# Delta rule: decay factors from running sums in zero-padded rows, values and gated outputs transposed by VectorE and through DRAM

## The chip, the cores and the metric

The kernel runs on one core of one Trainium2 chip. The metric is device time in microseconds (us), the median over runs of the whole program. Before the change it is 2708.5 us (three runs, 2707.7 to 2711.6). Engines are named as in the profile: PE is TensorE, PEld its weight load, DVE is VectorE, ACT is ScalarE, POOL is GpSimd, SP is SyncE, which issues nearly all DMAs. Line numbers (L354) are those of the kernel before; in the changed kernel they are a little different (the helper `tr`, L363, is L364 there, and `dma`, L367, is L368).

## The reference

Two pre-norm residual layers over 256 tokens of width 2048, all in float32. Layer 0 has stick-breaking attention as its mixer, layer 1 a gated DeltaNet; a SwiGLU FFN with 5632 hidden columns follows each. The change is in the second mixer:

```python
proj = h @ w_in                                   # q, k: 16 heads; v, z: 32 heads of 128
qkv, z, b, a = jnp.split(proj, [...], axis=-1)
qkv = jax.nn.silu(causal_dwconv(qkv, conv_w))     # 4 taps along the tokens, per channel
q, k = l2_norm(q) * dh ** -0.5, l2_norm(k)        # 16 heads, each used by two value heads
beta = jax.nn.sigmoid(b)
g = -jnp.exp(a_log) * jax.nn.softplus(a + dt_bias)
# in chunks, g the running sum inside a chunk:
decay = jnp.where(causal, jnp.exp(g[:, None] - g[None, :]), 0.0)
a_mat = strict_lower((k * beta) @ k.T * decay);  t_mat = inverse(a_mat + eye)
u, w = t_mat @ (v * beta), t_mat @ (k * beta * jnp.exp(g))
v_new = u - w @ state
out = (q * jnp.exp(g)) @ state + (q @ k.T * decay) @ v_new
state = state * jnp.exp(g_last) + (k * jnp.exp(g_last - g)).T @ v_new
o = rms_norm(out, o_norm) * jax.nn.silu(z)
y = o @ w_out
```

The kernel uses chunks of 128 tokens, so there are two (t = 0 and 1).

## The kernel before, in words

All 256 tokens stay on the chip. x is held as 128 tokens x 512 columns tiles; activations that feed a product are held transposed (channels on the partitions, 256 tokens along the row) as a pair hi, lo in the rounded type fp32r, with hi + lo the float32 value. Weights are streamed once from DRAM in *units* of two k-tiles (128 x 1024). SP loads a unit into a raw buffer, ScalarE writes its hi part, VectorE subtracts to get its lo part (L328, L332, tile `w`), and TensorE makes three products for each k-tile and half of the tokens: hi x hi, hi x lo, lo x hi. In the profile these are two matmuls on `w,hTh` and one on `w,hTl` (on `kh`, `kl` where the operand is an attention or FFN output), 128x512 each, into one of the accumulators `acc`. A block of 512 output columns over 16 k-tiles is 96 such matmuls. The FFNs use a seven-product scheme for part of their columns, with conversions of 128 x 1792.

**Order.** The program is one list in an order that the code plans itself; engines run their own part of it in sequence and wait on semaphores. The planner keeps a planned time for each engine (`self.t`). Weight blocks form the main stream; everything else is a *task*, a generator that does some instructions and yields. Before each group of three stream matmuls `tick` steps those tasks whose earlier instructions are done by the planned times, unless ScalarE or VectorE is planned more than `LAG` us past TensorE (`LAG7` in the FFN's seven-product part). `spend` adds an instruction's planned duration, `transfer` that of a DMA; `later` and `nap` postpone a task's next step. Nothing of these times exists on the chip: they only fix the order. `GDN_ORDER` lists the mixer's blocks: ('qk', g), ('v', g), ('z', g) for the eight groups g of four value heads, ('ba',) for the gates, ('out', a, b) for the product of heads a to b with w_out.

**Transposes.** There are two ways. `tr` (L363) lets TensorE transpose 128x128 by a product with the identity, into a PSUM bank. `turn` (L891) lets VectorE transpose a 128x512 tile in 32x32 blocks in place (STREAM_TRANSPOSE), writes it to a DRAM buffer `way` with stores of 32 partitions, and loads it back with two DMAs so that the blocks come out in their transposed places. If the two tiles lie side by side, four stores and two loads do; otherwise eight and two. Before, `turn` serves q and k of the attention and half of the norms (`TURNED`), and a like routine, `turned_pairs`, the FFN's hidden columns.

**The mixer's tasks, by group.** `gdn_qk`: evacuate, transpose on TensorE, convolve. `gdn_v`: evacuate two tiles (one for each t), transpose them by eight `tr` in two banks, convolve from the bank. `gdn_z`: evacuate, then Silu on z and on the convolved values; `gdn_values` transposes the values back. `gdn_scores` makes k k^T and k q^T, and multiplies them by the decay factors E that `gdn_decay` makes (which = 0 and 2: between positions of the first and of the second chunk; 1: from the start of the second chunk). `gdn_blocks32` and `gdn_inverse` invert, through DRAM scratch. `gdn_finish` applies all this to the values, normalises, multiplies by Silu(z) and has `transposed_pairs` turn the result (eight `tr` in two banks) and split it into `kh`, `kl` for the out blocks.

**Decay factors before.** `gdn_gates` puts g, token by token on the partitions, into `ghl` (hi and lo). For each group and t, VectorE multiplies the triangular mask `upto` by each head's g (tile `gm`, hi and lo, 128x512), and TensorE multiplies by the strict triangle `after` (or by ones for which = 1): six 128x512 matmuls for each group, which give the sums of g between two positions. ScalarE takes the exponential.

**Norm into the FFN.** `norm_part` transposes new x columns (by `tr` or `turn`), scales them into `hTh` and `hTl`, and spawns `norm_stats`, the squares of x (`slab<-x` on ScalarE). hTh_65 to hTh_79 (odd) and hTl_66 to hTl_80 are two k-tiles each; hTh_69 and hTl_70 hold k-tiles 4 and 5, of the second 512 columns.

Of the kernel before, what the change touches and what calls it, by code (L numbers as in the profile page):

```python
# [15 lines left out]
P = 128  # L16
D = 2048
S = 256
# [139 lines left out]
class Trunk:  # L158
# [16 lines left out]
    LAG = 2.0  # L175
# [9 lines left out]
    GDN_ORDER = [('qk', 0), ('ba',), ('v', 0), ('qk', 1), ('z', 0), ('v', 2), ('v', 1), ('z', 1), ('qk', 2), ('qk', 3), ('v', 3), ('z', 2), ('z', 3), ('out', 0, 4), ('out', 4, 8), ('qk', 4), ('v', 4), ('qk', 5), ('v', 5), ('z', 5), ('z', 4), ('qk', 7), ('v', 6), ('qk', 6), ('out', 8, 16), ('v', 7), ('z', 6), ('z', 7), ('out', 16, 24), ('out', 24, 32)]  # L185

    def __init__(self, ctx, tc, ins, out):
# [26 lines left out]
        self.scratch = [dram.tile(s, F32, name=f"scratch{k}") for k, s in enumerate(([32, 1024], [8, P * (P + 1)]))]  # L214
# [138 lines left out]
    def mm(self, out, lhsT, rhs, start=True, stop=True, after=0.0):  # L353
        self.nc.tensor.matmul(out, lhsT, rhs, start=start, stop=stop, skip_group_check=True)  # L354
# [64 lines left out]
    def more_constants(self):  # L419
# [16 lines left out]
        self.after = t("after", [P, P], F32R)  # L436
# [34 lines left out]
        self.copy(self.after, aft)  # L471
# [113 lines left out]
    def product(self, u):  # L585
        b, (hi, lo, after) = u.block, u.conv
        ks = range(u.k0, u.k0 + u.nk)
        if b.kind == "ba":
            acc = b.acc[0]
            c = b.cols  # L590
            for k in ks:
                o = b.ops[k]
                wh, wl = hi[:, k * c:(k + 1) * c], lo[:, k * c:(k + 1) * c]
# [297 lines left out]
    def turn(self, parts, back=False, src=None):  # L891
# [8 lines left out]
        self.cur.later = self.TURN  # L900
# [7 lines left out]
        for a in range(4):  # L908
# [10 lines left out]
            self.cur.nap = self.STEP if a < 3 else None  # L919
# [361 lines left out]
    def gdn_blocks(self, norm, nxt, last):  # L1281
# [13 lines left out]
        self.gs = [dict(g=g, ops=heads[4 * g:4 * g + 4]) for g in range(8)]  # L1295
        z0 = 2 * KEY + VAL
# [25 lines left out]
    def gdn_gates(self, acc, free):  # L1322
# [31 lines left out]
        gt = w[:, :, 0, :]  # L1354
        for t in range(NT):
            self.stt(gt[:, t, :], zz[:, t, 1, :], -1.0, ea, ALU.mult, ALU.mult)
        self.ghl = self.sb("ghl", [P, NT, 2, HV], F32R)
        for t in range(NT):
            self.act(self.ghl[:, t, 0, :], gt[:, t, :])
            self.tt(self.ghl[:, t, 1, :], gt[:, t, :], self.ghl[:, t, 0, :].bitcast(F32), ALU.subtract)  # L1360
# [4 lines left out]
        yield  # L1365

        self.rest = self.sb("rest", [P, HV])
        self.act(self.rest, bank[:, :HV], AF.Exp)
# [424 lines left out]
```

## Time and profile before

| | us |
|---|---|
| median of three runs | 2708.5 (2707.7 to 2711.6) |
| the profiled execution | 2705.98 |
| its span, first to last instruction | 2704.3 |
| PE busy | 2669.4 |
| DVE busy | 2182.7 |
| ACT busy | 1491.8 |
| DMA, share of 16 engines' time on queue q1 | 67.1% |

The span has four stretches: attention to about 405 us, the first FFN to 1080, the DeltaNet mixer to about 1980, the second FFN to the end. A group of the profile reads: line, engine, operation, output tile <- input tiles, shapes, count | busy us, mean ns of one | idle us of that engine just before, and what ended it. Matmul durations overlap (a 128x512 matmul shows as some 390 ns while the next one starts sooner), so the price of a matmul is read from the starts in a timeline, not from its duration. A row of a timeline has start, length, engine, line, operation, tiles, shape, count. A row of waits has: who waited <- for whom: us in total, times, longest us. A row of DMA issues ends with count, KB of one, and the median us from issue to landing.

### The profile page before, as it was taken

The numbers are of one execution on the slowest core, as the hardware profiler recorded it, in microseconds if no ns is written. First come the engines' busy times: TensorE is split into PE (matmuls) and PEld (weight loads), VectorE is DVE, ScalarE is ACT, GpSimd is POOL, SyncE is SP. The second block draws the span as 40 slices with busy tenths as digits, with TensorE's granted clock in tenths as the row PEclk, the third lists the DMA queues.
The fourth block names the chain that finished last, engine by engine and source line by source line (L and its number), as shares of the span: only waits on it lengthen the run. The fifth ranks groups of instructions, "written<-read, shape, count | busy, mean of one in ns | idle before, by whom it ended". The sixth has DMA issues, their size and how long they took to land.

```text
span 2704.3 us, 39527 instructions
## 1 busy us (share of the span) xinstructions
PE 2669.4 (99%) x14730; PEld 2274.6 (84%) x14730; DVE 2182.7 (81%) x3451; ACT 1491.8 (55%) x1961; POOL 11.2 (0%) x95
## 2 busy tenths in 40 slices
PE   9999999999999999999999999999999999999999
PEld 7888888888888888888888888888878888888887
DVE  6556568899999897678778887887679899989885
ACT  6555556554555554565665556645575555555453
POOL 0000000000000000000000000000000000000000
PEclk9999999999999999999999999999999999999999
DMA  7766775787676777855656556556567767767776
GB/s 245 202 185 196 219 211 164 208 231 212 203 218 205 208 211 233 227 174 172 182 143 195 159 161 175 168 153 186 170 191 212 223 196 220 217 188 218 226 209 188
DMA packets 487611, 534.41 MB, mean 198 GB/s; under 512 B 188087, under 2 KB 267258, under 8 KB 487418
## 3 DMA queue, kind: packets, MB, share of 16 engines
q1 hardware_dynamic: 487370, 531.87, 67.1%
q8 instruction: 115, 1.88, 0.3%
q14 instruction: 78, 0.64, 0.1%
q10 hardware_dynamic: 48, 0.02, 0.0%
HBM read 508.20 MB, written 23.59 MB: 197 GB/s over the span
## 4 chain that ended last, share of the span: by engine, by line
PE 83%; DVE 10%; issue 2%; ACT 2%; DMA 2%; SPq 0%; ACTq 0%; DVEq 0%
PE acc L354 61%; PE bank L354 20%; DVE w L332 5%; DVE slabs L332 2%; PE bank L363 1%; DMA slab<-in_ffn_w_gu_dram 1%; ACT slabs L328 1%; ACT w L328 1%; DVE slab L338 1%; DVE slab L332 1%; DVE slab L939 1%; DMA slab<-in_ffn_w_down_dram 0%; ACT slab L328 0%; DVE x L332 0%; DMA w<-in_ffn_w_gu_dram 0%
## 5 line engine op out<-in xcount | busy, mean ns | idle before, releaser
L332 DVE TENSOR_TENSOR w<-w,w 128x1024 fp32r<-128x1024 f32 (+2 forms) x746 | 946.3, 1285 | 249.0 <-ACT w L328 247.6
L328 ACT ACTIVATE w<-w 128x1024 fp32r<-128x1024 f32 (+2 forms) x650 | 802.8, 1244 | 417.8 <-PE acc L354 347.0
L354 PE MATMUL acc<-w,hTh 128*128 128x512 f32 (+1 forms) x3232 | 925.0, 369 | 9.1 <-DVE w L332 8.4
L354 PEld LDWEIGHTS acc<-w,hTh 128*128 128x128 f32 x3232 | 585.9, 189 | 120.5 <-DVE w L332 14.5
L354 PE MATMUL acc<-w,hTl 128*128 128x512 f32 (+1 forms) x1616 | 590.2, 365 | 3.1 <-DVE hTl L338 3.1
L328 ACT ACTIVATE slabs<-slab 128x1024 fp32r<-128x1024 f32 x264 | 279.3, 1058 | 431.9 <-DMA slab<-in_ffn_w_gu_dram 123.8
L332 DVE TENSOR_TENSOR slabs<-slab,slabs 128x1024 fp32r<-128x1024 f32 x264 | 321.5, 1218 | 93.1 <-ACT slabs L328 93.1
L354 PE MATMUL acc<-w,kh 128*128 128x512 f32 x1184 | 369.6, 393 | 0.0
L354 PEld LDWEIGHTS acc<-w,hTl 128*128 128x128 f32 x1616 | 304.5, 188 | 53.5 <-DVE hTl L338 3.9
L332 DVE TENSOR_TENSOR w<-w 128x256 f32<-128x256 f32 (+1 forms) x576 | 291.2, 508 | 9.8 <-DMA w<-in_ffn_w_gu_dram 2.6
L354 PEld LDWEIGHTS acc<-w,kh 128*128 128x128 f32 x1184 | 218.8, 188 | 43.7
L354 PE MATMUL acc<-w,kl 128*128 128x512 f32 x592 | 230.7, 390 | 0.0
L354 PE MATMUL acc<-slabs,hTh 128*128 128x512 f32 x608 | 190.1, 392 | 2.8 <-DVE slabs L332 2.8
L354 PE MATMUL bank<-w,wide 128*128 128x256 f32 x1296 | 178.9, 283 | 0.0
L354 PEld LDWEIGHTS bank<-w,wide 128*128 128x128 f32 x1296 | 165.8, 192 | 0.0
L354 PE MATMUL bank<-slabs,hTh 128*128 128x512 f32 x512 | 159.9, 392 | 3.1 <-DVE slabs L332 3.1
L354 PE MATMUL bank<-slabs,kh 128*128 128x512 f32 x512 | 159.6, 392 | 3.4 <-DVE slabs L332 3.4
L354 PE MATMUL acc<-slabs,kh 128*128 128x512 f32 x480 | 149.9, 392 | 2.1 <-DVE slabs L332 1.9
L354 PEld LDWEIGHTS acc<-slabs,hTh 128*128 128x128 f32 x608 | 111.0, 188 | 25.1 <-DVE slabs L332 4.9
L354 PEld LDWEIGHTS acc<-w,kl 128*128 128x128 f32 x592 | 111.1, 188 | 23.4
L354 PE MATMUL acc<-slabs,hTl 128*128 128x512 f32 x304 | 118.3, 389 | 0.0
L328 ACT ACTIVATE slab<-bank 32x128 f32<-32x128 f32 (+4 forms) x181 | 67.9, 379 | 89.3 <-PE bank L354 87.1
(216 smaller groups left out, 2933.4 us busy)
## 6 DMA issues: line engine op xcount, KB each, us to landing
w<-in_ffn_w_gu_dram SPq DMA_DIRECT2D x212, 512.0 KB, 4.5
slab<-in_ffn_w_gu_dram SPq DMA_DIRECT2D x140, 512.0 KB, 4.5
w<-in_gdn_w_in_dram SPq DMA_DIRECT2D x129, 512.0 KB, 4.3
slab<-in_ffn_w_down_dram SPq DMA_DIRECT2D x124, 512.0 KB, 4.5
w<-in_sb_w_in_dram SPq DMA_DIRECT2D x96, 512.0 KB, 4.5
w<-in_gdn_w_in_dram SPq DMA_DIRECT2D x128, 256.0 KB, 3.7
w<-in_gdn_w_out_dram SPq DMA_DIRECT2D x64, 512.0 KB, 4.4
w<-in_ffn_w_down_dram SPq DMA_DIRECT2D x52, 512.0 KB, 5.5
```

The source lines that it names most:

```text
L328: self.nc.scalar.activation(out, in_, func, **kw)
L332: self.nc.vector.tensor_tensor(out, a, b, op=op)
L338: self.nc.vector.scalar_tensor_tensor(out, a, s, b, op0=op0, op1=op1)
L354: self.nc.tensor.matmul(out, lhsT, rhs, start=start, stop=stop, skip_group_check=True)
L363: self.nc.tensor.transpose(out, in_, self.ident[:p, :p])
L939: self.nc.vector.transpose(s, t)
```

## The change

- *Decay factors.* `gdn_gates` lets TensorE form the running sums of g themselves, once for all heads, in both layouts: tokens on partitions (`gsum`) and heads on partitions. The latter goes as a hi and a lo row per head to a DRAM scratch. For each group `gdn_decay` loads two rows of 512 (hi and lo of four heads) and copies them into rows 0 and 1 of the tile `gm`, whose other 126 rows stay zero; one matmul with ones (`onesr`) spreads hi + lo over all partitions. ScalarE then makes exp(-relu(gsum - sum)): one Relu for each head with `gsum` as bias, one Exp. The products of VectorE and four of six matmuls per group are gone. `after` and `ghl` are gone.
- *Values.* `gdn_v` uses `turn` and convolves from the loaded tiles. `evac_tok` asks for two tiles side by side.
- *Gated outputs.* `gdn_finish` uses `turn` for all groups but that of the last z block in GDN_ORDER (group 7), which keeps the TensorE transposes.
- *Planning.* LAG is 3.0 instead of 2.0; a 128x512 fp32r matmul outside of the seven-product part is planned at 512/2400 + 0.0135 us instead of + 0.006; GDN_ORDER is another; the norm's `turn` waits 0.2 us instead of 1.0 before its stores and 0.5 instead of 1.2 between them (`soon`).

```diff
-    LAG = 2.0
+    LAG = 3.0
-    GDN_ORDER = [('qk', 0), ('ba',), ('v', 0), ('qk', 1), ('z', 0), ('v', 2), ('v', 1), ('z', 1), ...
+    GDN_ORDER = [('v', 0), ('ba',), ('qk', 1), ('qk', 0), ('v', 1), ('z', 1), ('z', 0), ('qk', 2), ...
...
         if lhsT.dtype == F32R:
-            self.spend("pe", max(0.107, n / 2400 + 0.006), after)
+            over = 0.006 if self.seven else 0.0135
+            self.spend("pe", max(0.101 + over, n / 2400 + over), after)
...
     def norm_part(self, st, n):
-            yield from self.turn(parts, src=[self.x[t][n] for t in range(NT)])
+            yield from self.turn(parts, src=[self.x[t][n] for t in range(NT)], soon=True)
...
     def turn(self, parts, back=False, src=None, soon=False):
-        self.cur.later = self.TURN
+        self.cur.later = 0.2 if soon else self.TURN
...
-            self.cur.nap = self.STEP if a < 3 else None
+            self.cur.nap = (0.5 if soon else self.STEP) if a < 3 else None
...
     def gdn_gates(self, acc, free):
+        s = yield from self.slabs.get()
+        gt = s[:, :NT * 2 * HV].rearrange("p (t k h) -> p t k h", t=NT, k=2)
...
-        for hl in range(2):
-            self.mm(bank[:, :HV], self.after, self.ghl[:, 0, hl, :], start=hl == 0, stop=hl == 1)
+        for t in range(NT):
+            self.mm(bank[:, t * HV:(t + 1) * HV], self.upto, gt[:, t, 0, :])
+            self.mm(bank[:2 * HV, S + t * P:S + (t + 1) * P], gt[:, t, :, :].rearrange("p k h -> p (k h)"), self.upto)
+        self.mm(bank[:, 2 * HV:3 * HV], self.negones, gt[:, 0, 0, :])
...
+        for k in range(2):
+            self.dma(self.scratch[2][k].rearrange("t h i -> h t i"), s[k * HV:(k + 1) * HV, :S].rearrange("h (t i) -> h t i", t=NT))
...
     def gdn_decay(self, G):
-        for t, outs in ((0, (0,)), (1, (2, 1))):
-            gm = yield from self.gms.get()
-            for hl in range(2):
-                gb = self.ghl[:, t, hl, gsl].bitcast(F32).unsqueeze(2).to_broadcast([P, 4, P])
-                self.tt(h4(gm[hl]), up, gb, ALU.mult)
-            yield
-            for which in outs:
-                bank = yield from self.banks.get()
-                lhs = self.onesr if which == 1 else self.after
-                for hl in range(2):
-                    self.mm(bank, lhs, gm[hl], start=hl == 0, stop=hl == 1)
-                yield
-                e = yield from self.slabs.get()
-                self.act(e, bank, AF.Exp)
+        for t in range(NT):
+            s = yield from self.slabs.get()
+            self.dma(s[0:2, :].rearrange("p (h i) -> p h i", h=4), self.scratch[2][:, t, 4 * g:4 * g + 4, :])
+            rows.append(s)
+        yield
+        gm = yield from self.gms.get()
+        for t in range(NT):
+            self.act(gm[t][0:2, :], rows[t][0:2, :])
+        self.slabs.put(*rows)
+        yield
+        for t in range(NT):
+            bank = yield from self.banks.get()
+            self.mm(bank, self.onesr, gm[t])
+            yield
+            e = yield from self.slabs.get()
+            for h in range(4):
+                n = slice(h * P, (h + 1) * P)
+                self.act(e[:, n], bank[:, n], AF.Relu, scale=-1.0, bias=self.gsum[:, t, 4 * g + h:4 * g + h + 1])
+            self.act(e, e, AF.Exp, scale=-1.0)
+            G["E"][2 * t] = e
+            if t == 1:
+                e = yield from self.slabs.get()
+                self.act(e, bank, AF.Exp)
+                G["E"][1] = e
...
     def gdn_v(self, G, acc, free):
         toks = yield from self.evac_tok(acc, free)
-        vc = []
+        yield from self.turn(toks)
+        G["vc"] = vc = yield from self.two()
         for part in range(2):
-            s = yield from self.slabs.get()
-            vc.append(s)
-            bank = yield from self.banks.get()
-            for j in range(2):
-                for t in range(NT):
-                    self.tr(bank[:, j * S + t * P:j * S + (t + 1) * P], toks[t][:, (part * 2 + j) * P:(part * 2 + j + 1) * P])
-            yield
-            self.conv([(bank[:, j * S:(j + 1) * S], s[:, j * S:(j + 1) * S], 32 + g * 4 + part * 2 + j) for j in range(2)])
+            halves = [slice(j * S, (j + 1) * S) for j in range(2)]
+            self.conv([(toks[part][:, n], vc[part][:, n], 32 + g * 4 + part * 2 + j) for j, n in enumerate(halves)])
...
     def gdn_finish(self, G):
-        yield from self.transposed_pairs(G["z"], G["ops"], self.gains[:, 66:67])
+        if g in self.gs_last:
+            yield from self.transposed_pairs(G["z"], G["ops"], self.gains[:, 66:67])
+            return
+        yield from self.turn(G["z"])
+        for n, s in enumerate(G["z"]):
+            pair = yield from self.pairs.get()
+            self.operands_of(G["ops"][2 * n:2 * n + 2], pair, s.rearrange("p (k s) -> p k s", k=2), self.gains[:, 66:67])
+        self.slabs.put(*G["z"])
```

How the order moves is shown at three places. The first is PE, the decay matmuls of the first groups in the mixer, between the products of a weight block (`acc`) with the last k-tiles; first before, then with the change.

```order
L354 MATMUL bank_109<-gm_95,after 128x512
L354 MATMUL bank_109<-gm_96,after 128x512
L354 MATMUL acc_105<-w_123,hTh_79 128x512 x2
L354 MATMUL acc_105<-w_123,hTl_80 128x512
L354 MATMUL bank_110<-gm_95,onesr 128x512
L354 MATMUL bank_110<-gm_96,onesr 128x512
L354 MATMUL acc_106<-w_123,hTh_65 128x512 x2
```

```order
L354 MATMUL bank_109<-gm_95,onesr 128x512
L354 MATMUL acc_105<-w_124,hTh_79 128x512 x2
L354 MATMUL acc_105<-w_124,hTl_80 128x512
L354 MATMUL bank_111<-gm_96,onesr 128x512
L354 MATMUL acc_106<-w_124,hTh_65 128x512 x2
```

gm_95 and gm_96 were hi and lo of one sum and are now the two chunks t, so that a pair becomes a single matmul, and the pairs with `after` have gone.

The second is ACT at the entry into the first FFN, where hTh_69 is made from the turned x (`slab,nss<-x_63` are the squares for the norm, `wide` operands of the seven-product scheme); first before, then with the change.

```order
L328 ACTIVATE slab<-bank_110,gains 128x256 x2
L328 ACTIVATE w_123<-w_122 128x1024
L328 ACTIVATE wide_2481<-slab 128x512
L328 ACTIVATE w_124<-w_122 128x1024
L328 ACTIVATE slab,nss_140<-x_63 128x512 x2
L328 ACTIVATE hTh_69<-slab,gains 128x256 x2
L328 ACTIVATE hTh_71<-slab,gains 128x256 x2
```

```order
L328 ACTIVATE hTh_75<-bank_111,gains 128x256 x2
L328 ACTIVATE w_124<-w_123 128x1024
L328 ACTIVATE slab<-bank_111,gains 128x256 x2
L328 ACTIVATE hTh_69<-slab,gains 128x256 x2
L328 ACTIVATE hTh_71<-slab,gains 128x256 x2
L328 ACTIVATE wide_2477<-slab 128x512
```

The squares of x_63 stood directly ahead of hTh_69 and now come eight rows behind it.

The third is SP in the mixer, after the gates' transfers, with the change (before, loads of `w` and the transfers of the inverse were all that stood there). way_122 is the DRAM buffer of the first group's values, scratch_116 that of the running sums.

```order
L368 DMA way_122<-slab 32x32x32
L518 DMA w_123<-in_gdn_w_in_dram 128x2x256 x2
L368 DMA way_122<-slab 32x32x32
L368 DMA scratch_116<-slabs 32x2x128 x2
L368 DMA way_122<-slab 32x32x32
L518 DMA w_123<-in_gdn_w_in_dram 128x2x256 x2
L368 DMA way_122<-slab 32x32x32
L518 DMA w_7759<-in_gdn_w_in_dram 128x2x256 x2
L518 DMA w_123<-in_gdn_w_in_dram 128x2x256 x2
L368 DMA slab<-way_122 128x4x128 x2
L518 DMA w_123<-in_gdn_w_in_dram 128x2x512 x3
```

Four stores and two loads of a turn now stand between the weight loads, and SP takes them in this sequence. The like happens for the other 14 turns.

More of the change, by code (lines that the diff above doesn't have):

```diff
@@ L213, in __init__ @@
         dram = ctx.enter_context(tc.tile_pool(name="scratch", bufs=1, space=bass.MemoryType.DRAM))
-        self.scratch = [dram.tile(s, F32, name=f"scratch{k}") for k, s in enumerate(([32, 1024], [8, P * (P + 1)]))]
+        self.scratch = [dram.tile(s, F32, name=f"scratch{k}") for k, s in enumerate(([32, 1024], [8, P * (P + 1)], [2, NT, HV, P]))]
         self.ways = Slots([dram.tile([NT * NB, P], F32, name=f"way{k}") for k in range(6)])
@@ L592, in product @@
                 o = b.ops[k]
+                if not o.ready:
+                    self.until(lambda: o.ready, ("operand", b.name, k))
                 wh, wl = hi[:, k * c:(k + 1) * c], lo[:, k * c:(k + 1) * c]
@@ L889, in two, with turn @@
         return [a, b]
-    def turn(self, parts, back=False, src=None):
+    def turn(self, parts, back=False, src=None, soon=False):
         way = yield from self.ways.get()
@@ L1295, in gdn_blocks @@
         self.gs = [dict(g=g, ops=heads[4 * g:4 * g + 4]) for g in range(8)]
+        self.gs_last = [item[1] for item in self.GDN_ORDER if item[0] == "z"][-1:]
         z0 = 2 * KEY + VAL
@@ L1369, in gdn_gates @@
         self.banks.put(bank)
+        self.sync()
+        self.act(self.rest, self.rest, AF.Exp, scale=-1.0)
+        for k in range(2):
+            self.dma(self.scratch[2][k].rearrange("t h i -> h t i"), s[k * HV:(k + 1) * HV, :S].rearrange("h (t i) -> h t i", t=NT))
+        yield
+        self.slabs.put(s)
+        for t in range(NT):
+            self.act(gm[t].rearrange("p (a i) -> p a i", a=4), self.upto[:, None, :].to_broadcast([P, 4, P]), scale=0.0)
+        self.gms.put(gm)
         self.flags.add("gates")
@@ L1372, in evac_tok @@
     def evac_tok(self, acc, free):
-        out = []
+        out = yield from self.two()
         for t in range(NT):
-            s = yield from self.slabs.get()
-            self.act(s, acc[t], scale=self.gn.rstd[:, t:t + 1])
-            out.append(s)
+            self.act(out[t], acc[t], scale=self.gn.rstd[:, t:t + 1])
         free()
@@ L1643, in gdn_v @@
         toks = yield from self.evac_tok(acc, free)
-        vc = []
+        yield from self.turn(toks)
+        G["vc"] = vc = yield from self.two()
         for part in range(2):
-            s = yield from self.slabs.get()
-            vc.append(s)
-            bank = yield from self.banks.get()
-            for j in range(2):
-                for t in range(NT):
-                    self.tr(bank[:, j * S + t * P:j * S + (t + 1) * P], toks[t][:, (part * 2 + j) * P:(part * 2 + j + 1) * P])
+            halves = [slice(j * S, (j + 1) * S) for j in range(2)]
+            self.conv([(toks[part][:, n], vc[part][:, n], 32 + g * 4 + part * 2 + j) for j, n in enumerate(halves)])
             yield
-            self.conv([(bank[:, j * S:(j + 1) * S], s[:, j * S:(j + 1) * S], 32 + g * 4 + part * 2 + j) for j in range(2)])
-            yield
-            self.banks.put(bank)
         self.slabs.put(*toks)
-        G["vc"] = vc
         self.flags.add(("vconv", g))
```

31 lines of the change are left out of this document (16 added, 15 removed).

## Prediction, on record before the changed kernel was timed

> **What bounds the kernel now.** I read the page first (busy shares, clock, chain of waits), then the busy time of each engine by stretch, then the waits of TensorE in the delta-rule stretch, and last single stretches of its timeline.
>
> ```profile
> PE 2669.4 (99%) x14730; PEld 2274.6 (84%) x14730; DVE 2182.7 (81%) x3451; ACT 1491.8 (55%) x1961; POOL 11.2 (0%) x95
> PE 83%; DVE 10%; issue 2%; ACT 2%; DMA 2%; SPq 0%; ACTq 0%; DVEq 0%
> core 0: us, PE busy (x) PEld busy (x) DVE busy (x) ACT busy (x) POOL busy (x), PEclk, DMA share, GB/s
> 405.00:1080.00 675.00, 663.54 (x3847) 583.99 (x3846) 603.49 (x780) 359.94 (x339) 0.53 (x1) 1.00 0.71 209
> 1080.00:1980.00 900.00, 899.62 (x5033) 740.15 (x5032) 707.37 (x1549) 529.53 (x934) 8.02 (x80) 1.00 0.61 177
> 1980.00:2600.00 620.00, 607.92 (x3572) 536.30 (x3571) 560.28 (x733) 336.56 (x318) 0.00 (x0) 1.00 0.71 207
> ```
>
> TensorE carries the chain (83%). The three stretches are the first FFN, the delta-rule layer's mixer, and the second FFN. In the FFNs TensorE is idle for 11.5 us (675 - 663.54) and 12.1 us (620 - 607.92), waiting for VectorE. In the mixer it is idle for 0.4 us in 900: there is no wait there to remove, and only work taken from TensorE can shorten it. The granted clock is 1.00 throughout. These are the waits: the first row is all that TensorE waits for between 1080 and 1980, the second is of the whole program.
>
> ```profile
> PE bank L363 <- ACT slab L328: 0.3, 1, 0.3
> PE acc L354 <- DVE hTl L338: 3.1, 2, 1.5
> ```
>
> A busy TensorE need not be a full one, so I looked at how its instructions start. Three weight matmuls (two with hTh, one with hTl) are the unit of the weight stream.
>
> ```profile
> 1342.57 0.39 PE L354 MATMUL acc<-w,hTl 128*128 128x512 f32 x1
> 1342.80 0.60 PE L363 MATMUL bank<-ident,slabs 128*128 128x128 f32 x4
> 1343.15 0.71 PE L354 MATMUL acc<-w,hTh 128*128 128x512 f32 x2
> 1343.70 0.39 PE L354 MATMUL acc<-w,hTl 128*128 128x512 f32 x1
> ...
> 1345.53 0.39 PE L354 MATMUL acc<-w,hTl 128*128 128x512 f32 x1
> 1345.76 0.62 PE L354 MATMUL acc<-w,hTh 128*128 128x512 f32 x2
> 1346.21 0.39 PE L354 MATMUL acc<-w,hTl 128*128 128x512 f32 x1
> ```
>
> From hTl to hTl the stream takes 0.68 us (1345.53 to 1346.21); with four transposes between, 1.13 us (1342.57 to 1343.70). Four transposes cost the stream 0.45 us, and nothing overlaps them.
>
> [...]
>
> **What the change takes from TensorE.** Values: 8 transposes per group of four heads in gdn_v, 64 in 16 runs of four. Gated outputs: 8 in gdn_finish for all groups but the last (7), 56 in 14 runs of four. 30 runs x 0.45 = **-13.5 us**. The price of a run next to other side work differs little: the transposes themselves start 0.11 us apart.
>
> Decay factors: six 128x512 matmuls per group become two.
>
> ```profile
> 1196.54 0.62 PE L354 MATMUL acc<-w,hTh 128*128 128x512 f32 x2
> 1196.99 0.40 PE L354 MATMUL acc<-w,hTl 128*128 128x512 f32 x1
> 1197.23 0.62 PE L354 MATMUL bank<-gm,after 128*128 128x512 f32 x2
> 1197.69 0.63 PE L354 MATMUL acc<-w,hTh 128*128 128x512 f32 x2
> ...
> L354 PE MATMUL bank<-gm,after 128*128 128x512 f32 x32 | 10.7, 414 | 0.0
> L354 PE MATMUL bank<-gm,onesr 128*128 128x512 f32 x16 | 5.3, 412 | 0.0
> ```
>
> From hTh to hTh it is 1.15 us with a pair (1196.54 to 1197.69), so the pair costs 1.15 - 0.68 = 0.47, one matmul 0.235. 48 matmuls become 16: 32 x 0.235 = **-7.5 us**.
>
> Gates: two 128x32 matmuls go, five small ones in full fp32 come (two of them 64x128). The nearest row is one full-fp32 128x128 matmul, two records each:
>
> ```profile
> 1388.13 0.38 PE L354 MATMUL bank<-slab,wide 128*128 128x128 f32 x2
> 1388.35 0.39 PE L354 MATMUL bank<-slabs,wide 128*128 128x128 f32 x2
> ```
>
> 0.22 us each; five are at most 1.1 us, and what goes is some 0.2. I take **+0.6** (bounds 0.2 and 1.1).
>
> **What it moves to other engines.**
>
> ```profile
> L332 DVE TENSOR_TENSOR gm<-upto,ghl 128x512 fp32r<-128x512 f32 x32 | 20.5, 680 | 0.0
> L897 DVE STREAM_TRANSPOSE slab<-x 128x512 f32<-128x512 f32 x8 | 5.2, 684 | 0.0
> L332 DVE TENSOR_TENSOR w<-w,w 128x1024 fp32r<-128x1024 f32 x270 | 325.0, 1217 | 97.8 <-ACT w L328 96.9 <-DMA w<-in_gdn_w_in_dram 0.3
> L328 ACT ACTIVATE w<-w 128x1024 fp32r<-128x1024 f32 x270 | 280.4, 1055 | 119.5 <-PE acc L354 115.5 <-DVE w L332 2.2 <-issue 1.2
> L325 ACT ACT_TABLE_LOAD x25 | 32.1, 1283 | 0.4
> L328 ACT ACTIVATE slab<-bank 128x128 f32<-128x128 f32 x36 | 9.5, 278 | 10.1 <-PE bank L354 10.1
> L328 ACT ACTIVATE slab<-slab 128x512 f32<-128x512 f32 x26 | 15.4, 622 | 3.3 <-DVE slab L338 3.2
> ```
>
> VectorE loses 32 products of 0.68 (-21.8 us) and gains 30 transposes of 0.684 (+20.5): even. ScalarE gains 64 Relu of 128x128 (0.278: +17.8) and 16 copies of two rows of 512 (0.622 by the row of that length: +10.0) and loses four table loads (-5.1): about +22.7 us, from 529.5 to 552 of some 880. Neither sets the end while weight conversions keep ahead, and they do: ScalarE's conversions wait 115.5 us for TensorE to free a buffer (0.43 us for each of 270), VectorE's wait for ScalarE, and almost never for a load (0.3 us). If that cover is gone, each us lost on either engine is a us of TensorE. Convolution and splitting into hi and lo are the same operations with an SBUF source: no charge.
>
> DMA gains 94 transfers for the 15 turns (14 with six, one with ten), 16 small loads of decay rows and two stores.
>
> ```profile
> way<-slab SPq DMA_DIRECT2D x144, 128.0 KB, 5.3
> slab<-way SPq DMA_DIRECT2D x72, 256.0 KB, 5.0
> SPq L367 <- DMA way<-slab: 19.5, 12, 4.2
> ACT kh L328 <- DMA slab<-way: 25.2, 14, 5.0
> L328 ACT ACTIVATE hTh<-slab,gains 128x256 fp32r<-128x256 f32 x12 | 5.1, 496 | 1.0 <-DMA slab<-way 1.0
> ```
>
> A turn takes 5.3 us from its last store and 5.0 us for its loads, over 10 us where PE transposes took 0.45. The users are not near: one block of 512 columns is 96 weight matmuls (16 k-tiles x 2 x 3), 32 x 0.68 = 21.8 us, and values wait for their group's z block anyway, which stands a block or more later. What can be hit is what is queued behind: SP holds a turn's load until its stores have landed (12 times, 1.6 us mean, 4.2 at most), with weight loads behind it; ScalarE reaches the turned tile early and holds the conversions behind it. In the FFNs that happened 14 times (1.8 us mean, 5.0 at most). In this stretch the same kind of turn, made for the norm, held ScalarE 1.0 us in all. So each turn costs between 0 and 1.8 us minus cover; nearest is the norm's turn, so I take **+2.5 us** for 15 turns, the row loads and the new order together (bounds 0 and 12, beyond that the first rival).
>
> [...]
>
> **Order and waiting times.** LAG 3 instead of 2 lets side work start with up to 1 us more queued on ScalarE and VectorE; the matmul's planned time rises, and the new GDN_ORDER and shorter pauses of the norm's turn move side work. In the attention stretch only places shift by one or two threes: nothing. At both entries into an FFN something can be won.
>
> ```profile
> 404.00 0.61 ACT L328 ACTIVATE slab<-x 128x512 f32<-128x512 f32 x1
> 404.74 0.63 ACT L328 ACTIVATE slab<-x 128x512 f32<-128x512 f32 x1
> 405.37 1.70 ACT L328 ACTIVATE hTh<-slab,gains 128x256 fp32r<-128x256 f32 x4
> ```
>
> Two squares of x_63 (404.00 to 405.37) stand ahead of hTh_69, for whose remainder hTl TensorE then waits 1.5 us, at both entries (3.1 us, second row of waits). The change puts them behind it. 1.37 us earlier each covers most of that wait: **-2.5 us** (bounds -3.1 and +1).
>
> **Sum.** -13.5 - 7.5 + 0.6 + 2.5 - 2.5 = -20.4 us. The profiled execution took 2705.98 us (span 2704.3 and 1.7 around it) and comes to 2685.6. The median of the runs is 2708.5, 2.5 above it; I forecast **2688 us** for the median. The bounds together give 2708.5 - 20.8 - 3.1 = 2684.6 at the low end, and with +12, +1 and 1.1 in place of the middle values 2708.5 - 21.0 + 14.1 = 2701.6 at the high end.
>
> **Rivals.**
> 1. The turns stop the conversions (slower). If every turn held ScalarE for the FFN's mean (1.8 us) and SP as well (1.6 us), less the slack that ScalarE's conversions show on average (0.43 us for each, two in a turn's time: 0.8), 15 x 2.6 = 39 us in place of 2.5: 2688 - 2.5 + 39 = about **2724**. It is slower than before from 1.6 us a turn (23 / 15). For it: the FFN's rows. Against: the norm's turns in this same stretch, and 115.5 us in which ScalarE waited for TensorE.
> 2. VectorE becomes a bound in the mixer as in the FFNs. With LAG 3 side work goes in larger heaps ahead of conversions. If TensorE lost the share that it loses in the first FFN (11.5 / 675 = 1.7%) on some 880 us, 15 us in place of 2.5: about **2700**. For it: VectorE is busy 79% of the mixer (707.37 / 900). Against: in the FFN it is 89% (603.49 / 675), and its total does not rise here.
> 3. The work does not leave the path because other side work fills the place: nothing speaks for it, the removed matmuls are counted, and I leave it out.
>
> **How the numbers follow.** The forecast's own case has 0.79 (2684 to 2695), rival 2 0.13, rival 1 0.08. The range 2680 to 2703 holds the first and most of the second; its low end allows 4 us below the bounds for entries and waits that I priced singly. A change within 0.2% (5.4 us) can hardly be told from none. Faster by more: 0.79 + 0.09 of rival 2 = 0.88; within it: 0.04 of rival 2 and 0.02 of rival 1 = 0.06; slower: 0.06.
>
> **What would show it.** Right: the groups of transposes on slab and slabs lose 120 of 258, gm with onesr stays at 16 and gm with after is gone; the mixer's stretch is some 18 to 20 us shorter with TensorE idle under 3 us; TensorE's wait for hTl at the FFN entries under 1 us. Wrong: new rows of TensorE waiting for w of VectorE or ScalarE in the mixer; ScalarE rows on slab or kh that wait for slab<-way over 15 us in all; SP held long by way<-slab with weight loads landing late. If the time falls by less than 15 us with no such rows, the price of a transpose was wrong.

## The result: 1.0% slower

The changed kernel takes 2736.1 us (median of six runs, 2726.1 to 2744.4), the kernel before 2709.5 (2707.7 to 2711.6): a ratio of 1.0096 (95% interval 1.0071 to 1.0122). The forecast was 2688 us. Its runs also spread over 18 us, those of the kernel before over 4. Four single executions of the runs below took 3281 to 9937 us and count in no median or ratio here. The profiled execution has a span of 2731.1 us, 26.8 more than before.

The page of the changed kernel (busy times, and the chain of waits by engine):

```profile
PE 2668.1 (98%) x14586; PEld 2264.3 (83%) x14586; DVE 2181.9 (80%) x3450; ACT 1515.1 (55%) x2040; POOL 11.2 (0%) x95
PE 70%; DVE 15%; ACT 5%; DMA 5%; issue 4%; SPq 1%; ACTq 0%; DVEq 0%; POOL 0%; POOLq 0%
```

TensorE's share of the chain fell from 83% to 70%; VectorE, ScalarE and DMA came in its place. Outside its busy time TensorE had 34.9 us before (2704.3 - 2669.4) and has 63.0 now (2731.1 - 2668.1): 28.1 us more idle time. The mixer, and all that TensorE waits for there:

```profile
1080.00:1980.00 900.00, 875.64 (x4801) 714.39 (x4800) 694.95 (x1525) 542.34 (x991) 7.95 (x80) 0.98 0.66 188
...
PE bank L354 <- DVE slab L1640: 6.0, 3, 5.4
PE acc L354 <- DVE w L332: 5.4, 4, 3.4
PE bank L364 <- ACT slab L328: 3.1, 3, 1.5
PE acc L354 <- DVE x L332: 2.6, 2, 2.5
PE bank L354 <- ACT slab L328: 2.6, 1, 2.6
PE bank L354 <- ACT slabs L328: 2.1, 2, 1.1
PE bank L354 <- DVE slabs L332: 1.7, 1, 1.7
```

Where TensorE was idle for 0.4 us in 900, it is idle for 24.4. Most rows are on `bank`: side work put into the order of TensorE at a place where its input was not there yet. And the clock, 1.00 before, is 0.98. In steps of 3.4 us (the columns are busy times; the clock is the third number from the end):

```profile
1844.00:1847.40 3.40, 2.44 (x11) 1.69 (x9) 1.72 (x2) 2.31 (x3) 0.00 (x0) 1.00 1.08 315
1847.40:1850.80 3.40, 0.00 (x0) 0.00 (x0) 1.77 (x3) 1.15 (x2) 0.00 (x0) 1.00 1.11 340
1850.80:1854.20 3.40, 2.35 (x34) 2.16 (x35) 2.68 (x4) 2.08 (x5) 0.00 (x0) 0.50 1.13 308
1854.20:1857.60 3.40, 3.40 (x54) 2.42 (x53) 2.60 (x7) 1.51 (x6) 0.00 (x0) 0.50 1.03 233
1857.60:1861.05 3.45, 3.45 (x13) 2.41 (x14) 1.22 (x1) 2.12 (x5) 0.16 (x1) 0.50 1.12 346
1861.05:1864.50 3.45, 3.45 (x23) 2.60 (x22) 2.18 (x6) 2.24 (x4) 0.00 (x0) 1.00 0.70 111
```

A wait of 5.4 us is followed by three windows of 3.4 us at half clock. Eight such windows, in five places, make 27.3 us at half clock, which loses up to 13.7 us (mean clock 0.995, 0.005 x 2731.1). More idle time and half clock together are some 42 us; the time rose by 26.8, so by busy time the work itself fell by about 15, where the forecast took away 20.4 (13.5, 7.5 and 0.6 the other way). Busy time hides some idle time: a 128x512 matmul ahead of a wait shows as 0.39 us, where the next one would have started after 0.227. Counted from the starts instead (each TensorE instruction at the mean distance to the next start that its kind has in the kernel before where no wait follows), the work is 2661.7 us before and 2641.9 now, 19.8 less.

The chains into the three longest waits of the mixer (2.6, 5.4 and 3.4 us), in order of time (start, us, what), first the two with a DMA in them:

```profile
1761.64 7.42 DMA slab<-way
...
1769.77 0.70 ACT kh L328
...
1770.50 0.87 ACT slab L328 x2
...
1771.41 0.38 PE bank L354
```

```profile
1842.18 6.58 DMA w<-in_gdn_w_in_dram
...
1848.86 1.06 ACT w L328
...
1849.95 1.22 DVE w L332
1851.17 0.63 DVE slab L1640
...
1851.85 0.25 PE bank L354
```

In the first, a turn's load lands 7.4 us after its issue (5.0 before); ScalarE stands at `kh` until then, with the copies behind it for which TensorE waits. In the second a weight load takes 6.6 us; ScalarE's and VectorE's conversions wait for it, and behind VectorE's stands a transpose of the inverse. The third one (3.4 us, at 1596.02) has no DMA in it: VectorE has six convolution products (2.4 us) and eight steps of the inverse ahead of a conversion.

```profile
1590.13 2.37 DVE slab L338 x6
...
1594.83 1.14 DVE w L332
...
1596.02 0.79 PE acc L354
```

In the mixer ScalarE now waits for turns and late weights, and the DMA engines move half again as many packets (the first fence is of the change, up to 2008 us, the second of before, its packets up to 1985):

```profile
ACT kh L328 <- DMA slab<-way: 14.8, 4, 5.1
ACT slab L328 <- DMA slab<-way: 11.4, 3, 5.5
ACT w L328 <- DMA w<-in_gdn_w_in_dram: 11.0, 4, 4.8
...
DMA packets 222690, 176.72 MB, mean 190 GB/s; under 512 B 106499, under 2 KB 167555, under 8 KB 222615
```

```profile
ACT hTh L328 <- DMA slab<-way: 1.0, 2, 0.6
...
DMA packets 144338, 160.20 MB, mean 177 GB/s; under 512 B 43472, under 2 KB 89552, under 8 KB 144264
```

One of the four waits at `kh`, 4.3 us at 1079.5 us, is for a turn of the first FFN; the fifteen new turns hold ScalarE six times, for 21.9 us (10.5 at `kh`, 11.4 at `slab`).

Not all of the loss is in the mixer. The last matmul on `kl` of the attention starts at 404.33 us in place of 399.59 (+4.7), that of the mixer at 2005.45 in place of 1979.84 (+25.6).

### The profile page after: what moved, and what is told of

It is laid out like the page before. It is cut to its first block, busy times and chain, and to the rows that moved or that the text cites. A ratio compares the mean times of both kernels' runs of the same rounds, so it can differ in the third digit from the quotient of the medians.

```text
span 2731.1 us, 39496 instructions
## 1 busy us (share of the span) xinstructions
PE 2668.1 (98%) x14586; PEld 2264.3 (83%) x14586; DVE 2181.9 (80%) x3450; ACT 1515.1 (55%) x2040; POOL 11.2 (0%) x95
## 4 chain that ended last, share of the span: by engine, by line
PE 70%; DVE 15%; ACT 5%; DMA 5%; issue 4%; SPq 1%; ACTq 0%; DVEq 0%; POOL 0%; POOLq 0%
PE acc L354 49%; PE bank L354 20%; DVE w L332 7%; DVE slabs L332 3%; ACT w L328 2%; ACT slab L328 1%; DVE slab L332 1%; DVE slab L338 1%; DMA slab<-way 1%; ACT slabs L328 1%; DMA slab<-in_ffn_w_gu_dram 1%; DMA way<-slab 1%; SPq L368 1%; DVE slab L940 1%; PE bank L364 1%
## 5 line engine op out<-in xcount | busy, mean ns | idle before, releaser
L354 PEld LDWEIGHTS bank<-slabs,kh 128*128 128x128 f32 x512 | 93.3, 188 | 21.9 <-DVE slabs L332 4.7
```

## The experiments

Three theories stood at the start: **A**, the turns' transfers; **B**, the planning constants and the new order; **C**, the decay's new steps. From e10 on a fourth, **S**: that TensorE waited for nothing before belongs to that one order, and any other loses time. The table has each run's median, its ratio to the kernel before with its interval, and from its profiled execution the time outside TensorE's busy time (34.9 us before) and the loss by half clock, (1 - mean clock) x span (an upper bound, since some of it falls into idle time, and good to some 1.5 us, since the clock is given to three digits). The profiled executions of e8, e9, e14 and e17 lie 5 to 8 us above the medians of their runs. Differences in the text are to the median of the kernel before in the same round of runs (2708.0 to 2709.5).

| run | median us | ratio (95%) | idle us | half clock us |
|---|---|---|---|---|
| the change | 2736.1 | 1.0096 (1.0071 to 1.0122) | 63.0 | 13.7 |
| e1 plan alone | 2738.9 | 1.0111 (1.0091 to 1.0131) | 51.7 | 2.7 |
| e2 turns alone | 2778.9 | 1.0259 (1.0245 to 1.0273) | 100.7 | 47.2 |
| e3 decay alone | 2719.4 | 1.0039 (1.0025 to 1.0053) | 44.0 | 8.1 |
| e4 plan and decay | 2745.4 | 1.0142 (1.0124 to 1.0160) | 59.1 | 11.0 |
| e5 LAG 3 alone | 2723.9 | 1.0050 (1.0037 to 1.0062) | 44.9 | 5.4 |
| e6 planned rate alone | 2713.1 | 1.0015 (1.0006 to 1.0024) | 38.9 | 0 |
| e7 GDN_ORDER alone | 2729.2 | 1.0076 (1.0063 to 1.0088) | 52.0 | 8.2 |
| e8 change, LAG 2 | 2745.7 | 1.0134 (1.0120 to 1.0148) | 79.6 | 19.2 |
| e9 before, relieved | 2700.9 | 0.9965 (0.9953 to 0.9977) | 44.0 | 10.8 |
| e10 change, no transfers | 2713.0 | 1.0013 (1.0004 to 1.0022) | 51.0 | 2.7 |
| e11 before, LAG 2.1 | 2739.0 | 1.0106 (1.0092 to 1.0120) | 50.2 | 19.2 |
| e12 change, LAG 3.1 | 2734.6 | 1.0094 (1.0080 to 1.0108) | 60.8 | 10.9 |
| e13 decay, LAG 2.4 | 2711.0 | 1.0009 (1.0000 to 1.0018) | 38.1 | 2.7 |
| e14 decay, LAG 2.2 | 2725.0 | 1.0060 (1.0047 to 1.0072) | 48.2 | 16.4 |
| e15 before, LAG 1.9 | 2750.3 | 1.0153 (1.0140 to 1.0166) | 60.2 | 22.0 |
| e16 change, loads aside | 2728.9 | 1.0071 (1.0059 to 1.0083) | 59.1 | 8.2 |
| e17 decay, LAG 4 at the end | 2715.3 | 1.0023 (1.0012 to 1.0033) | 44.1 | 10.9 |
| e18 decay, LAG 6 at the end | 2717.7 | 1.0031 (1.0019 to 1.0043) | 46.5 | 2.7 |

**The parts alone.** e1 is the kernel before with these edits:

```diff
-    LAG = 2.0
+    LAG = 3.0
-    GDN_ORDER = [('qk', 0), ('ba',), ...
+    GDN_ORDER = [('v', 0), ('ba',), ...
-            self.spend("pe", max(0.107, n / 2400 + 0.006), after)
+            over = 0.006 if self.seven else 0.0135
+            self.spend("pe", max(0.101 + over, n / 2400 + over), after)
     (and soon=True for the norm's turns)
```

One more edit of the planner belongs to the change, and is in e1 to e4 and in the runs made from them or from the change: before a matmul of the main stream it steps tasks until the operand has been made (`if not o.ready: self.until(...)`). Its share was not measured by itself.

> The kernel before with the planning part of the change alone: LAG 3, the matmul's planned time 0.0135, the new GDN_ORDER, the shorter pauses of the norm's turns. Every value, gated output and decay factor is made as before. The change gave +26.8 us where -20.4 us was forecast, so some 47 us are to be found. Theory A (the turns: their transfers land late, hold ScalarE and delay weight loads): 2704 to 2714 us, TensorE idle in the mixer under 4 us. Theory B (the plan: more side work ahead of the conversions on VectorE): 2730 us or more, idle in the mixer over 10 us. Theory C (the decay's new steps on ScalarE and the row loads): as A, 2704 to 2714.

2738.9 us: the plan alone costs 31 us, as B said; A and C expected none.

e2 has the two turns alone (`yield from self.turn(toks)` in gdn_v, `yield from self.turn(G["z"])` in gdn_finish, two tiles side by side in evac_tok), e3 the new gates and decay alone, e4 the plan and the decay:

> The kernel before with the two turns alone (values of all eight groups, gated outputs of seven); order, LAG, planned times and decay as before. The transposes that go are worth 13.5 us. Theory A: 2709 - 13.5 + some 40 = about 2735 us, with TensorE idle in the mixer for 20 us and records of ScalarE and VectorE that wait for a turn's load or a late weight load. Theory B or C: 2696 to 2702 us, idle under 4 us. In either case the granted clock falls to 0.5 behind each idle stretch of over some 2.5 us and nowhere else.

> The kernel before with the new gates and decay factors alone; order, LAG, planned times and transposes as before. 32 matmuls of 0.235 us less and some 0.6 us more. Theory A or B: 2709 - 7 = 2702 us (2699 to 2705), idle in the mixer under 2 us. Theory C: over 2715 us, with conversions late behind the rows' loads.

> The whole change but for the turns: values and gated outputs are transposed by TensorE as before. Theory A: 2709 - 7 - 2 = about 2700 us (2696 to 2706). Theory B: over 2720 us. If the parts add up, this is e1 plus e3 less the time before.

e2 is worst of all with 2778.9, beyond what A expected. The longest waits of TensorE in its mixer, up to 2010 us:

```profile
PE acc L354 <- ACT kh L328: 31.0, 4, 14.5
PE bank L354 <- DVE gm L332: 15.1, 3, 10.6
```

TensorE itself stands at out blocks for ScalarE's `kh`; in the longest of these waits (14.5 us) ScalarE stands 11.3 us for a turn's load. Half clock starts within three of the four, and also behind a wait of 1.5 us that ends at 2058.8 us, which the expectation (only behind waits of over some 2.5 us) ruled out; in the change four of the five half-clock stretches stand behind waits of 2.5 to 5.4 us. e3 does not come to 2702 but to 2719.4, though C explains little of it: conversions wait for a load for 4.1 us in all. TensorE is idle in its mixer for 10.2 us, 4.6 of them from 1924 to 1944 us, where the clock is at half besides (more on that at e11). e4 comes to 2745.4, near e1 plus e3 less the time before (2750); the three parts are no sum all the same: plan, turns and decay alone cost 31, 71 and 11 us, together 27. Without the plan the turns cost more, and without the turns the plan costs as much as the whole change. A, B and C each explain a part, and none the whole.

**The plan taken apart.** e5, e6, e7 change one line each of the kernel before, e8 puts LAG = 2.0 into the changed one.

> The kernel before with LAG 3 in place of 2 and nothing else. The plan alone cost 31 us (2738.9 against 2708.0), and it is now taken apart. Theory B1 (LAG: up to 1 us more side work may be queued on ScalarE and VectorE ahead of a conversion): 2725 us or more, TensorE waiting for w of VectorE in the mixer. Theory B2 (the planned rate of TensorE) or B3 (the order of the blocks): 2705 to 2712 us.

> The kernel before with the matmul's planned time alone: 0.0135 in place of 0.006 outside the seven-product stretches. A weight matmul is planned at 0.2268 us in place of 0.2193; the traces show 0.227. With 0.006 the plan holds TensorE for 3% faster than it is, so side work and conversions come out that much thinner than the chip could take them: a reserve. Theory B2 (that reserve is gone): 2720 us or more, and the attention stretch some 4 us longer, as in e1. Theory B1 or B3: 2705 to 2712 us.

> The kernel before with the new GDN_ORDER alone. Theory B3 (blocks whose side work is heavy come closer together, and work for one group meets that of another): 2720 us or more, with the attention stretch unchanged. Theory B1 or B2: 2703 to 2712 us.

> The changed kernel with LAG 2 in place of 3 and nothing else (its median was 2736). Theory B1: some 20 us less, 2705 to 2718 us. Theory B2 or B3: 2728 to 2745 us; with the turns, less may then be started per pause, which could also hold the turns back and cost a few us.

LAG 3 costs 15 us, the planned rate 4, GDN_ORDER 20. B3 holds and B1 all but holds (1 us short of its 2725), where each expected the other not to, and B2's price was far too high. But the same LAG 3 that costs 15 us in the kernel before is worth some 10 in the changed one (e8 is slower than the change, though the two intervals touch). So LAG 3 is not bad by itself, as S says.

**What the removed work is worth, what the transfers cost, and two controls.** e9 leaves instructions of the kernel before in place and only drops some; e10 does so with the changed kernel's transfers:

```diff
 e9, gdn_v, transposed_pairs (not group 7), gdn_decay
-                    self.tr(bank[...], toks[t][...])
+                    self.spend("pe", 0.107)
-                    self.mm(bank, lhs, gm[hl], start=hl == 0, stop=hl == 1)
+                    if hl == 0: self.mm(bank, lhs, gm[hl], start=True, stop=True)
+                    else: self.spend("pe", max(0.107, NB / 2400 + 0.006))
 e10, turns of gdn_v and gdn_finish: dma() plans the transfer, but issues none
-        self.nc.sync.dma_start(out, in_)
+        if not still:
+            self.nc.sync.dma_start(out, in_)
 e11, e12
-    LAG = 2.0            -    LAG = 3.0
+    LAG = 2.1            +    LAG = 3.1
```

> The kernel before with every instruction in its old place, and 120 transposes (64 of the values, 56 of the gated outputs) and 24 decay matmuls (the second of each pair) simply left out on TensorE, with nothing put in their place; values, gated outputs and decay factors are then not what they should be. It measures what the work that the change takes from TensorE is worth by itself. Theory P (the price in the prediction: 30 x 0.45 + 24 x 0.235 = 19.1 us, conversions keep ahead): 2709 - 19 = 2690 us, idle in the mixer under 3 us. Theory R (conversions and inputs of side work have little reserve, so that TensorE, once shortened, waits for them): 2697 us or more, with the difference as idle time in the mixer.

> The changed kernel (2736 us) with every instruction in its place but the 94 transfers of the fifteen turns left out; values and gated outputs stay transposed in 32x32 blocks only. Nothing waits for a turn, and SP and the DMA engines carry none. Theory A (the transfers: late landing, and weight loads late behind them): 2715 us or less, the idle stretches at ScalarE's kh and at the late weight load gone. Theory S (the new order loses its time on VectorE and ScalarE by itself): 2726 us or more, idle in the mixer still over 15 us.

> A control: the kernel before with LAG 2.1 in place of 2.0. The work is the same and the limits hardly differ, but the order written out shifts in many places. Theory S (that TensorE waits for nothing in the mixer belongs to that one order; any other loses 5 to 25 us in waits and in half clock behind them): 2714 to 2735 us. If the parts of the change did the harm by what they are: 2705 to 2712 us.

> The same control on the changed kernel: LAG 3.1 in place of 3.0. Theory S: it moves by more than 5 us from 2736, one way or the other, with other idle stretches than those of the change. If the change's loss is that of its transfers and steps as such: 2731 to 2741 us with the same idle stretches.

e9 comes to 2700.9: 8 us (6 to 13 by the interval) of the 19 that leave TensorE come back, with no transfer, no new step and no other order. Its profiled execution, the slowest of its six, shows where the rest goes (5.2 us idle in the 900, and two places there at half clock, of which one is shown):

```profile
1080.00:1980.00 900.00, 894.78 (x4923) 734.09 (x4922) 713.59 (x1561) 533.08 (x942) 8.00 (x80) 0.99 0.60 179
...
PE bank L354 <- DVE slab L1616: 4.4, 3, 2.3
...
1287.60:1291.00 3.40, 1.91 (x35) 1.44 (x35) 2.13 (x3) 0.54 (x2) 0.00 (x0) 1.00 1.09 261
1291.47:1294.88 3.41, 3.41 (x31) 2.37 (x30) 0.13 (x1) 2.09 (x5) 0.16 (x1) 0.50 1.06 281
1294.88:1298.30 3.42, 3.42 (x9) 2.64 (x8) 2.94 (x15) 0.93 (x1) 0.00 (x0) 0.50 0.49 162
```

With transposes gone TensorE reaches the inverse's small matmuls before VectorE has made their input (`DVE slab L1616`, the inverse's transpose). Theory R holds for the time; of the loss, idle time in the mixer is one part and half clock, in the mixer and behind it, another.

e10 comes to 2713.0: the 94 transfers cost 23 us, good to some 7 by the spread of the change's runs. The time is A's (2715 or less) and not S's; but TensorE is still idle in the mixer for 14.6 us, and the time is 4 us above the kernel before with some 20 us of work less. That rest is the order's and that of the other new steps; e10 doesn't separate them.

e11 is the control for S: LAG 2.1 in place of 2.0, the same work, costs 30 us, more than S itself expected and far from the 2705 to 2712 us of the other side. Most of that is one place at the end of the mixer:

```profile
1929.61 0.40 PE L354 MATMUL acc<-w,kl 128*128 128x512 f32 x1
1929.84 0.27 PE L363 MATMUL bank<-ident,slab 128*128 128x128 f32 x1
1934.74 1.75 PE L363 MATMUL bank<-ident,slab 128*128 128x128 f32 x7 [4.63 <-DVE slab L338]
1942.19 0.87 PE L354 MATMUL bank<-slab,wide 32*32 32x32 f32 x16 [5.70 <-DVE slab L1610]
...
1948.59 2.07 PE L354 MATMUL bank<-slab,slabs 128*128 128x128 f32 x8
...
1965.54 1.22 PE L354 MATMUL acc<-w,kh 128*128 128x512 f32 x2
```

From 1929.6 to 1965.5 us no weight matmul runs: the next out block needs a group that isn't finished, and what is left of it is a chain over all engines, at half clock from 1932 on (eight 128x128 records take 2.07 us; at full clock, in the change at 1766.41 us, 1.06). By the plan's prices the stretch is 12.4 us of work (10.6 by the distances between starts in the kernel before); it takes 36. So 23 to 25 of the 30 us are lost here. This can be seen in the order written out, ahead of any run: the orders of the kernel before and of the change have no stretch of side work over 4.3 us there, those of e2, e3, e7 and e11 one of 7 to 12 us.

e12 moves by 1.5 us only, within the noise, though its long waits are elsewhere (6.3 us at a `kh` at 1444 us, 3.3 us at 1753). S expected over 5: for the changed kernel it did not show. Nor does S fit e6, whose new order costs only 4 us.

**Where the two causes lie.** e13 and e14 are e3 with another LAG, e15 the kernel before with LAG 1.9; e16 keeps all transfers of the change and turns their loads aside:

```diff
-                self.dma(parts[n].rearrange("p (k c) -> p k c", k=2), ...
+                self.dma(self.void(aside, S * n, "(c t) j -> c (t j)"), ...      (a DRAM buffer that nobody reads)
```

> The decay part alone (as e3, 2719.7 us) with LAG 2.4. In e3 the order written out has, near the end of the mixer, one stretch of 12.4 us of TensorE side work (the last group's inverse and what follows it) with no weight matmul between; with LAG 2.4 it has none over 4.3 us. Theory T (that bare stretch is where e3 lost its time: each small matmul there waits for the step before it, at half clock): 2697 to 2707 us, the 7 us of removed matmuls showing. Theory S (any new order loses 5 to 25 us in many small waits): 2712 us or more.

> The same with LAG 2.2, whose order has no bare stretch over 4.3 us either. Theory T: 2697 to 2707 us, as e13. Theory S: 2712 us or more, and apart from e13 by over 5 us.

> The kernel before with LAG 1.9. Its order has a bare stretch of 16.6 us at the end of the mixer (e11: 12.4 us; the kernel before: none over 4.3 us). Theory T: 2730 to 2750 us, with TensorE at half clock for over 20 us around 1930. Theory S: anywhere from 2714 to 2740, and the loss spread over the mixer.

> The changed kernel with every instruction in its place, the turns' stores too, but their 30 loads go into DRAM that nobody reads; values and gated outputs stay transposed in 32x32 blocks. All 94 transfers are still issued and moved, and SP still waits for the stores, but ScalarE waits for no turn. Left out altogether the transfers were worth 23 us (e10: 2713 against 2736). Landing (ScalarE and what is queued on it waits for a turn's load): 2713 to 2720 us. Load (SP and the DMA engines are busy with turns, so weight loads and other loads come late): 2726 to 2738 us.

e15 is 41 us slower, at the upper end of T's range, at half clock for 27 us from 1943 on: of the two controls the one with the longer bare stretch is slower, as T says. Its stretch takes 49.7 us (1928.0 to 1977.7) for the 16.6 planned, so 33 of the 41 us are lost there. e13 (2711.0) lies between the theories and e14 (2725.0) with S: without the bare stretch the time is lost elsewhere (in e14 half clock for 17 us from 1684 on). e16 comes to 2728.9, 16 us above e10: that much of the 23 is traffic (with the reservation that a load into DRAM isn't quite the load that it replaces). The other 7 would be waits for the landing, but the runs of e16 (2724.6 to 2732.4) overlap with those of the change (2726.1 to 2744.4), so these 7 are not clear of the noise. In the mixer the DMA engines are busy for 0.60 of the time without the transfers and 0.67 with them turned aside (e10, then e16):

```profile
1080.00:1980.00 900.00, 885.40 (x4885) 723.52 (x4884) 705.74 (x1547) 551.17 (x1006) 7.96 (x80) 1.00 0.60 177
```

```profile
1080.00:1980.00 900.00, 878.25 (x4831) 715.44 (x4831) 699.40 (x1532) 545.97 (x994) 7.94 (x80) 0.99 0.67 190
...
ACT w L329 <- DMA w<-in_gdn_w_in_dram: 7.2, 4, 3.8
```

ScalarE's waits for late weights (7.2 us in the last row, 11.0 in the change, none in e10) stay with the loads aside.

**A version that beats both** was sought in the decay part, the cheapest one:

```diff
+                self.LAG = getattr(u.block, "lag", 2.0)
...
+            for b in blocks[was:]:
+                b.lag = 4.0 if n >= len(self.GDN_ORDER) - 9 else 2.0      (e18: 6.0, the last 7)
```

> The decay part alone (e3) with LAG 2 as before, but 4 for the last nine blocks of GDN_ORDER. Up to there the order is that of e3, whose weight conversions ran some 14 to 18 us ahead of those of the kernel before late in the mixer and then lost 25 us at the end. The bare stretch of 12.4 us is gone (none over 4.3 us). Theory T: 2695 to 2703 us, faster than the kernel before. Theory S: the freed side work now stands ahead of conversions and loses elsewhere what the end wins, 2709 us or more.

> The same with LAG 6 for the last seven blocks. Theory T: 2695 to 2703 us. Theory S: 2709 us or more, since up to 6 us of side work may then be queued ahead of a conversion.

2715.3 and 2717.7: S again. That e3's conversions ran ahead late in the mixer seems to have been no gain, only side work put off; no run shows this by itself. No kernel here that does all the work is faster than the one before.

## Why the prediction was wrong

1. **The step that failed is "there is no wait there to remove, and only work taken from TensorE can shorten it".** It was read as if every us of work taken away came back, in a new order as in the old one. e9 tests it alone: 8 of 19. Idle time of 0.4 us did not mean that the other engines had a reserve; it meant that in this order they were just in time. The reserve was argued from sums (115.5 us in which ScalarE's conversions wait for TensorE, 0.43 us for each of 270). In the change the same waits sum to 121.9 us, and TensorE waits all the same: mostly on inputs of side work, for which no reserve had been read at all. In sum, the forecast and the measurement are 47 us apart (-20.4 against +26.6). The transfers are 21 of these (23 against the 2.5 forecast, e10); the other 26 are there without the transfers, as idle time and half clock of the shortened and re-planned program, for which the sum had no term.
2. **The prices of what is removed** were about right. The transposes on `slab` and `slabs` fall from 258 to 138, `gm,onesr` stays at 16, and the work, counted from the starts, falls by 19.8 us against 20.4 forecast. By busy time it is 15, for the reason given above; e1, which removes nothing, comes out the same by starts as the kernel before (2661.8 us), though its busy time is 8.7 us longer.
3. **The turns: +2.5 us, bounds 0 and 12.** Measured 23 (change against e10). The nearest row was that of the norm's turns, with 1.0 us of waits; ScalarE's waits for the new turns are 21.9 us now, and some 16 of the 23 are traffic, for which the sum had no term. "The users are not near" was wrong: ScalarE came three times to turned values and three times to turned gated outputs before they had landed. Rival 1 named the mechanism and priced it at 39 us (its limit of 1.6 us a turn, 23 / 15, should read 1.5). So 23 us for the transfers stand against 13.5 for the transposes.
4. **Order: "the new order together" inside the +2.5, and the attention at nothing.** The plan alone costs 31 us in the kernel before (e1). The attention is 4.7 us longer; TensorE waits there twice for a turn's load, 2.7 us in all, and the planned rate gives 1.3 us (e6: last `kl` at 400.93). Some of it differs from run to run: with the same order there, the last `kl` starts at 402.24 in e10 and at 403.08 in e16.
5. **FFN entries: -2.5 us.** The wait for hTl (1.5 us at each entry) is gone, as said. But the conversions behind it are then late: up to 460 us TensorE waits 2.9 us for `w` in place of 1.0. Nothing was won. (The first row answers to point 4; the last is of the kernel before, in a fence of its own.)

```profile
PE bank L354 <- DMA slab<-way: 2.7, 2, 1.5
...
PE acc L354 <- DVE w L332: 2.9, 3, 1.2
```

```profile
PE acc L354 <- DVE w L332: 1.0, 1, 1.0
```

6. **Rival 2** (heaps on VectorE, +15 us) was seen too, at 1590 to 1596 us, and e5 gives just that for LAG 3 in the kernel before; in the changed kernel LAG 3 is the better value (e8).
7. **Half clock was in no term.** The granted clock of 1.00 was read as a fact about the kernel; of the profiled executions here only those of the kernel before and of e6, with 34.9 and 38.9 us idle, have a mean of 1.000. Half clock costs up to 13.7 us here, up to 22 in e15 and 47 in e2.
8. The chance of slower, 0.06, and the upper end of 2703 left out that the waits of several causes add up, and that half clock follows some of them (four waits of the mixer in the change).

## What to carry to other kernels

Where an order written by a planner shows a bound engine with no idle time, that is a property of this order and says nothing of a reserve on the other engines: before counting a removed instruction as time, look for what must arrive earlier once it is gone, on every input of the side work, and price a re-planned order by a control that changes nothing but the order (here LAG 2.1: 30 us). Count transfers as traffic as well as latency (here 16 of 23 us, e16). A stretch of side work without stream work under it can be counted in the order before the run, and may cost three times its matmuls (36 us for 12.4 in e11).

## What the hardware showed

In the traces of the kernel before and of the change the granted clock of TensorE shows two values, 1.00 and 0.50. In the change its five half-clock stretches start at 1349.05, 1506.07, 1594.81, 1772.31 and 1850.81 us and last for 3.41, 3.41, 6.83, 3.41 and 10.24 us, that is 1, 1, 2, 1 and 3 times 3.413; the distances between their starts are 46, 26, 52 and 23 times 3.413. A step of 3.413 us on this grid is called a window here. In the windows just ahead of these stretches TensorE was busy for 3.12, 1.00, 1.20, 0.89 and 0.00 us. At the first FFN entry of e11 half clock stands behind a window with a wait of 1.5 us:

```profile
406.40:409.80 3.40, 1.83 (x10) 1.13 (x9) 3.37 (x7) 3.40 (x8) 0.00 (x0) 1.00 0.46 140
409.80:413.20 3.40, 3.40 (x10) 2.62 (x9) 3.40 (x6) 3.27 (x8) 0.00 (x0) 0.50 0.50 160
```

The same wait in the kernel before (1.53 us, of which 0.05 fell into the next window) had none behind it; nor had one of 1.57 us there, from 691.67 us on, that lay in one window whole (TensorE busy for 1.84 of 3.41 us; the windows there are counted back from 2705.28 us, where the clock falls after the last instruction). In the change a wait of 1.71 us that ends at 1706.64, in a window with TensorE busy for 1.70 us, had none either. So busy time does not decide it alone: ahead of the first half-clock stretch of the change (1349.05) TensorE was busy for 3.12 of 3.41 us and waited for 0.29, and of its 3.12 us some 2 were matmuls of 32x32 and 128x1. At the end of the mixer in e3 the clock stayed at 0.50 though TensorE looks busy (some matmuls of 32x32 ahead of it, then 64x64 and 128x128 in full fp32, with waits between; one window, busy for 2.59 us, is left out):

```profile
1923.60:1927.05 3.45, 1.72 (x49) 1.50 (x49) 1.47 (x3) 1.94 (x7) 0.00 (x0) 1.00 0.41 135
1927.05:1930.45 3.40, 3.40 (x24) 3.26 (x24) 0.32 (x1) 1.52 (x5) 0.00 (x0) 0.50 0.00 0
1930.45:1933.90 3.45, 3.32 (x18) 2.71 (x16) 0.02 (x1) 0.97 (x2) 0.00 (x0) 0.50 0.00 0
...
1937.30:1940.70 3.40, 3.40 (x18) 3.40 (x18) 0.50 (x3) 1.63 (x11) 0.00 (x0) 0.50 0.00 0
```

Ahead of half clock TensorE was busy for 1.2 us of 3.4 in the second place of e9 (1731.80 to 1735.20), for 1.8 in e11 and for 1.7 in e3. So the wait of 1.5 us in e11 cost up to 1.7 us more (an estimate: half of the 3.40 us at half clock that follow it); what in a window decides, no run here shows.
